# Sixteen taps of a second convolution group on TensorE, and the convolution's norm moved forward, in a two-layer streaming encoder

## The chip, the cores and the metric

The kernel runs on one core of a Trainium2 chip. The metric is the device time of one execution in microseconds; the median of several runs is given. The core has four engines that compute: TensorE (PE, with its weight loads PEld listed apart), VectorE (DVE), ScalarE (ACT) and GpSimd (POOL). SyncE (SP) only issues transfers here.

## What is computed

Two layers of a Conformer-like block over 512 tokens of width 1024: half a feed-forward block, a mixing block, half a feed-forward block, a norm. The mixing block projects the normed input once; part of the columns goes to an attention with low-rank queries and keys, the other part to a convolution module. Both results are joined and go through one output projection. The change is in the convolution module and what follows it:

```python
def conv_group(u_raw, conv_w, conv_b, ln_g, ln_b):
    a, g = u_raw[..., :CONV_W], u_raw[..., CONV_W:]
    u = a * jax.nn.sigmoid(g)
    y = lax.conv_general_dilated(u, conv_w[:, None, :], window_strides=(1,),
        padding=[(CONV_K - 1, 0)], feature_group_count=CONV_W, ...)   # depthwise, 31 taps, causal
    y = y + conv_b
    return jax.nn.silu(layer_norm(y, ln_g, ln_b))                     # norm over the 512 channels
...
x = x + jnp.concatenate([attn, conv], axis=-1) @ w_out[l]
```

## The kernel before

The stream `x` stays on the chip as eight tiles of 128 features by 512 tokens. Matrix products with weights are done in three parts (high x high, high x low, low x high, helper `mm3`, lines 158 to 160), so each block of 128 x 128 weights costs three matmuls over 512 tokens. The feed-forward blocks, which the change does not touch, fill most of the time.

The mixing block (`mix_body`) runs once per layer. The 512 convolution channels are four groups c = 0 to 3 of 128. `conv_in(c)` makes the gated input `u[c]` of a group (its last step is L640). The list `TAPS = (0, 31, 31, 0)` divides the 31 taps of each group between engines:

- groups 0 and 3: all taps on DVE, one `scalar_tensor_tensor` per tap into one PSUM bank (L956, tag `cv`, one bank for both groups one after the other), then a copy to SBUF by ACT (L964);
- group 1: a product per tap on ACT (L960, tile `pr`, four buffers) and an add per tap on POOL (L962);
- group 2 (`PC`): the first 16 taps on TensorE in `conv_pe` (L664), the other 15 as in group 1. For TensorE, `u[2]` is copied with shifts of 0 to 3 tokens by 16 transfers on SP's queue (L656) into four tiles `shifted`; 16 matmuls with diagonal 32 x 32 blocks (`diag`) then sum 16 taps, each a pair of records in the trace; ACT takes the result out with the bias (L666).

Attention goes over eight heads in a software pipeline. At step k it issues the transposes `turn(k)` (L836, L841), `scores(k-1)` (L860, maxima on DVE L864, exponents on ACT L868), `turn_p(k-3)` (L883, L886) and, for two heads at a time, `values` (L898, L901, L905, L908) and `turn_out`, which splits a result into high and low parts (L165, L166). `conv_pe` is put in front of step `PSTEP = 3`.

After the heads comes the convolution's norm over the 512 channels: the sum `ysum` of the four group results, two adds on POOL (L978, L979) and one on DVE (L980), in a buffer from the five shared `tmp` tiles; the mean by a matmul (L982); a subtraction per group (L988); squares on ACT (L188, L191) with adds on DVE (L195); the sum over channels by one-column matmuls (L202); the power -1/2 on POOL (L177); a diagonal on DVE (L217) that a matmul spreads to all channels (L221); a product per group (L998), the swish on ACT (L1000), and the split. The tables of ACT's functions are loaded for the exponents at L923 and for the swish at L984.

The output projection has eight column blocks, each a group of 8 x 3 matmuls: four over attention's results (`at`), four over the convolution's (`cv`). The attention halves of the first four blocks (`early_groups`) are issued between the steps of the norm.

The order on each queue is fixed when the program is built: a planner goes through a simulated timeline and gives an engine, at each moment, the ready instruction that comes first in the program (or has a higher priority). On the chip each queue runs in that order.

Of the kernel before, what the change touches and what calls it, by code (L numbers as in the profile page):

```python
# [15 lines left out]
P = 128  # L16
# [21 lines left out]
NP = 3  # L38
NC = 2
CHUNKS = ((0, 2), (2, 5), (5, 8), (8, 11))  # L40
TAPS = (0, 31, 31, 0)
Q = 32
PT = 16
PC = 2
PSTEP = 3
AHEAD = 2
PAUSE = 16
SEQ = "q0 R c1 q1 q2 qo k kt tt uq uk c2 c3"
# [3 lines left out]
EARLY = "s"  # L52
PRELOAD = 1
E1 = 1
E2 = 2
E3 = 3
WOG = 4
WAKE = 10
KS = (0, 2, 4, 6, 1, 3, 5, 7)
WOP = 4  # L60
# [2 lines left out]
JOINED = ("b21", "t3", "t4")  # L63

VECS = [("g1", 8), ("gm", 8), ("g2", 8), ("gp", 8), ("gql", 3), ("gkl", 2),
        ("cw", 4 * CK), ("cb", 4), ("lg", 4), ("lb", 4), ("gq", 1), ("gk", 1), ("cp", PT)]
VOFF = {}
_o = 0
for _n, _w in VECS:
# [9 lines left out]
def encoder_kernel(ctx: ExitStack, tc: tile.TileContext, xT, consts, vecs, rgain, wgu1, wd1, wdq1,  # L79
# [11 lines left out]
    def nm(s):  # L91
        uid[0] += 1
        return f"{s}{uid[0]}"
# [4 lines left out]
    def tmp(w=S, dt=FP):  # L98
        return tmps.tile([P, w], dt, tag="t", name=nm("t"))

    def bank():
        return psum.tile([P, S], FP, tag="ps", name=nm("ps"))

    def tiny(tag, w, dt=FP):
        return small.tile([P, w], dt, tag=tag, name=nm(tag))
# [73 lines left out]
    class Stats:  # L179


        def __init__(self):
            self.acc = self.tail = None

        def add(self, src, scale=1.0, last=False, eng=None, apart=False):
            if self.acc is None:
# [7 lines left out]
                return  # L194
            (eng or (V if last else G)).tensor_tensor(self.acc, self.acc, sq, ALU.add)  # L195

        def sums(self):
            ps = bank()
            parts = [self.acc] + ([self.tail] if self.tail is not None else [])
            for part in parts:  # L200
                for t in range(NT):
                    order["sums"] = T.matmul(ps[:, t:t + 1], part[:, t * P:(t + 1) * P], ones[:, 0:1],  # L202
                                             start=part is self.acc and (t == 0 or len(parts) == 1),
                                             stop=part is parts[-1], skip_group_check=len(parts) > 1).ins
            return ps[:, 0:NT]

        def token(self, n):
            self.ve = small.tile([P, NT], FP, tag="vtok", name=nm("vtok"), bufs=4)
            V.tensor_scalar(self.ve, self.sums(), 1.0 / n, EPS, ALU.mult, ALU.add)
# [4 lines left out]
    def spread(r):  # L214

        dg = tmp()
# [3 lines left out]
        ps = bank()  # L220
        order["spread"] = T.matmul(ps, ones, dg, start=True, stop=True).ins  # L221
        return ps

# [396 lines left out]

    def mix_body(kpool, l, gx, norm, done):
        u, order = [], {}
        diag = kpool.tile([P, PT, Q], FP, tag="m", name=nm("m"), bufs=11)
        G.tensor_tensor(diag, cst[:, None, CI32:CI32 + Q].to_broadcast([P, PT, Q]),
                        vv(l, "cp")[:, :, None].to_broadcast([P, PT, Q]), ALU.mult)
        shifted = []

        def kept(dt=FP):
            return kpool.tile([P, S], dt, tag="m", name=nm("m"), bufs=11)
        ys = [kpool.tile([P, S], FP, tag=f"y{c}", name=nm("y"), bufs=1) if n else None for c, n in enumerate(TAPS)]  # L630

        def glu(pa, pg):
            tg = tmp()
# [9 lines left out]
        def conv_in(c):  # L643
            pp = []
            for j in range(2):
                ps = bank()
                group(ps, load_w(wcv[l, 2 * c + j], WC, f"c{c}"), gx, range(KD), KD)
                pp.append(ps)
            glu(*pp)
            if c != PC:  # L650
                return
            for i in range(4):
                v = slot()
                V.memset(v[:, 0:4], 0.0)
                for r in range(4):
                    nc.sync.dma_start(out=v[r * Q:(r + 1) * Q, r:], in_=u[c][i * Q:(i + 1) * Q, 0:S - r])  # L656
                shifted.append(v)

        def conv_pe():

            ps = bank()
            for a in range(PT // 4):
                for i in range(4):
                    T.matmul(ps[i * Q:(i + 1) * Q, 4 * a:], diag[:, 4 * a + i], shifted[i][:, 0:S - 4 * a],  # L664
                             start=a == 0, stop=a == PT // 4 - 1)
            A.activation(ys[PC], ps, AF.Identity, bias=vv(l, "cb")[:, PC:PC + 1])  # L666

        gql, gkl = vv(l, "gql"), vv(l, "gkl")
        KW = KVL + DR
# [176 lines left out]
        def scores(h):  # L846
            qT, kT = heads[h]["qk"]
            b01, b2, b3 = bank(), bank(), bank()
            if h % 2 == 0:
                heads[h]["sums"] = small.tile([P, NT, 2], FP, tag="sums", name=nm("sums"), bufs=3)  # L850
            sums = heads[h - h % 2]["sums"]
            mx = small.tile([P, NT], FP, tag="mx", name=nm("mx"), bufs=3)
            pi = []
            ps = [slot() for _ in range(3)]
            ps = [ps[0][:, 0:128], ps[0][:, 128:384], ps[1][:, 0:384], ps[2]]
            for i in range(NT):
                n = (i + 1) * P
# [10 lines left out]
                A.activation(p, o, AF.Exp, bias=mx[:, i:i + 1], scale=scqs[i][:, h:h + 1] if QFOLD else 1.0,  # L868
                             accum_out=sums[:, i, h % 2:h % 2 + 1])
                pi.append(p)  # L870
            heads[h]["p"] = pi

# [70 lines left out]
        cw, cb = vv(l, "cw"), vv(l, "cb")  # L943
        for c, n in enumerate(TAPS):
            tap = lambda k: cw[:, c * CK + k:c * CK + k + 1]
            acc = psum.tile([P, S], FP, tag="cv", name=nm("cv"), bufs=1) if n < CK else None
            if n and c != PC:
                A.activation(ys[c], u[c], AF.Identity, scale=tap(CK - 1), bias=cb[:, c:c + 1])
            for s in range(n, CK):
                k = CK - 1 - s  # L950
# [3 lines left out]
                    A.activation(acc[:, s:], u[c][:, :S - s], AF.Copy, scale=tap(k))  # L954
                else:
                    V.scalar_tensor_tensor(acc[:, s:], u[c][:, :S - s], tap(k), acc[:, s:], ALU.mult, ALU.add)  # L956
            for s in range(PT if c == PC else 1, n):
                k = CK - 1 - s
                pr = kpool.tile([P, S], FP, tag="pr", name=nm("pr"), bufs=4)
                A.activation(pr[:, s:], u[c][:, :S - s], AF.Copy, scale=tap(k))  # L960
                with tc.issue_after(order["keys"]) if s >= PAUSE or c > 1 else nullcontext():
                    order["conv"] = G.tensor_tensor(ys[c][:, s:], ys[c][:, s:], pr[:, s:], ALU.add).ins  # L962
# [15 lines left out]
        G.tensor_tensor(ysum, ys[0], ys[1], ALU.add)  # L978
        G.tensor_tensor(ysum, ysum, ys[2], ALU.add)  # L979
        V.tensor_tensor(ysum, ysum, ys[3], ALU.add)  # L980
        pm = bank()
        T.matmul(pm, onesm, ysum, start=True, stop=True)  # L982
        if PRELOAD:
            A.activation(tiny("pre", 1), ysum[:, 0:1], AF.Silu)  # L984
# [293 lines left out]
```

## Time and profile before

| what | value |
|---|---|
| median of 3 runs | 1805.45 us (1805.23 to 1808.48) |
| the profiled execution | 1807.3 us, its span 1805.5 us |
| mean granted TensorE clock | 0.995 |
| PE busy in the span | 99% |
| DVE, ACT, POOL busy | 83%, 61%, 21% |
| the DVE steps of the taps (L956) | 120, 88.0 us busy |
| the POOL steps of the taps (L962) | 90, 120.7 us busy |

All times of the trace count from the start of the span. A row of the timeline gives start, length, engine, line, operation, and in brackets how long the engine was idle before and what ended that. A matmul is pipelined and its end is modelled, so a busy PE need not be a full one. The first mixing block lies at about 300 to 560 us, the second at about 1195 to 1455.

### The profile page before, as it was taken

The page shows a single profiled execution, that of the slowest core. Times are in us where ns is not written, and L with a number is a line of the kernel's source. Part 1 is how long each engine was busy: PE and PEld are TensorE (multiplying, and loading weights), DVE is VectorE, ACT ScalarE, POOL GpSimd, SP SyncE. Part 2 cuts the span into 40 slices and gives each one's busy share as a digit, 9 for nine tenths or more (in the row PEclk, how much of TensorE's full clock was granted, in tenths as well). Part 3 has the DMA queues.
Part 4 walks back from the last instruction along what each step waited for, and adds up shares of the span by engine and source line. Part 5 has one row for each costly group of instructions (what it writes and reads, how often), then busy time and mean ns, then how long its engine had stood idle before and what let it go on. Part 6 is the DMA issues. An engine that isn't in the chain of part 4 may idle for free.

```text
span 1805.5 us, 29455 instructions
## 1 busy us (share of the span) xinstructions
PE 1786.9 (99%) x11430; PEld 1585.0 (88%) x11430; DVE 1497.1 (83%) x2309; ACT 1094.3 (61%) x1699; POOL 381.4 (21%) x313
## 2 busy tenths in 40 slices
PE   9999999999999999999999999999999999999998
PEld 7899999888668899999888999998976788999997
DVE  7898988689945989898779989876998559989883
ACT  5575756467843575756645656554777435757564
POOL 1000000258623000000310000002685310000002
PEclk9999999999999999999999999999999999999999
DMA  4657574325203466665426575743260125575742
GB/s 167 167 135 188 128 182 116 107 88 134 54 12 111 115 163 161 158 158 135 123 64 169 125 191 125 191 108 117 74 174 3 36 88 159 142 177 138 179 120 73
DMA packets 71947, 228.28 MB, mean 126 GB/s; under 512 B 8448, under 2 KB 9600, under 8 KB 71808
## 3 DMA queue, kind: packets, MB, share of 16 engines
q1 hardware_dynamic: 55536, 171.87, 29.8%
q0 software_dynamic: 16128, 54.53, 17.6%
q8 instruction: 89, 1.46, 0.3%
q14 instruction: 50, 0.41, 0.1%
q10 hardware_dynamic: 144, 0.00, 0.0%
HBM read 222.19 MB, written 2.10 MB: 124 GB/s over the span
## 4 chain that ended last, share of the span: by engine, by line
PE 90%; DVE 4%; ACT 3%; POOL 1%; issue 1%; DMA 0%; SPq 0%; ACTq 0%; DVEq 0%; POOLq 0%
PE ps L158 23%; PE ps L160 23%; PE ps L159 23%; PE ps L377 11%; PE ps L378 6%; ACT pr L960 1%; PE ps L905 1%; ACT r L868 1%; PE ps L860 1%; PE ps L883 1%; PE ps L202 1%; POOL sck L177 1%; PE ps L898 0%; PE ps L221 0%; DVE kn L810 0%
## 5 line engine op out<-in xcount | busy, mean ns | idle before, releaser
L159 PE MATMUL ps<-r,wh 128*128 128x256 f32 (+1 forms) x2556 | 814.7, 319 | 0.5 <-DVE r L166 0.5
L158 PE MATMUL ps<-r,wh 128*128 128x256 f32 (+1 forms) x2556 | 811.6, 321 | 3.5 <-ACT r L165 1.5
L160 PE MATMUL ps<-r,wl 128*128 128x256 f32 (+1 forms) x2364 | 757.0, 322 | 0.0
L158 PEld LDWEIGHTS ps<-r,wh 128*128 128x128 f32 x2556 | 484.4, 190 | 50.1 <-ACT wh L142 3.4
L159 PEld LDWEIGHTS ps<-r,wh 128*128 128x128 f32 x2556 | 485.5, 190 | 37.5 <-DVE r L166 2.6
L160 PEld LDWEIGHTS ps<-r,wl 128*128 128x128 f32 x2364 | 449.0, 190 | 34.8 <-DVE wl L148 0.7
L377 PE MATMUL ps<-xj,wh 128*128 128x512 f32 x864 | 303.8, 391 | 0.0
L142 ACT CAST wh<-raw 128x1024 fp32r<-128x1024 f32 (+3 forms) x148 | 132.4, 901 | 210.2 <-PE ps L159 126.5
L248 ACT CAST wh<-fr 128x1024 fp32r<-128x1024 f32 (+1 forms) x160 | 157.6, 985 | 105.1 <-DVE fr L414 49.4
L148 DVE TENSOR_TENSOR wl<-raw,wh 128x1024 fp32r<-128x1024 f32 (+3 forms) x132 | 144.6, 1103 | 89.3 <-ACT wh L142 88.6
L394 POOL DMA_DIRECT2D ls<-in_wgu x72 | 62.5, 868 | 734.6 <-ACT ls L393 501.7
L250 DVE TENSOR_TENSOR wl<-fr,wh 128x1024 fp32r<-128x1024 f32 (+1 forms) x160 | 182.0, 1138 | 20.1 <-ACT wh L248 20.1
L377 PEld LDWEIGHTS ps<-xj,wh 128*128 128x128 f32 x864 | 161.4, 188 | 30.1
L378 PE MATMUL ps<-xj,ls 128*128 128x256 f32 x576 | 161.3, 280 | 0.0
L962 POOL TENSOR_TENSOR y<-y,pr 128x495 f32<-128x495 f32 (+29 forms) x90 | 120.7, 1342 | 46.6 <-ACT pr L960 41.0
L248 ACT CAST wh<-raw 128x1024 fp32r<-128x1024 f32 (+1 forms) x100 | 98.2, 982 | 45.3 <-PE ps L159 24.5
L250 DVE TENSOR_TENSOR wl<-raw,wh 128x1024 fp32r<-128x1024 f32 (+1 forms) x100 | 113.4, 1134 | 14.3 <-ACT wh L248 13.8
L378 PEld LDWEIGHTS ps<-xj,ls 128*128 128x128 f32 x576 | 108.3, 188 | 0.0
L393 ACT ACTIVATE ls<-fr 128x1024 fp32r<-128x1024 f32 (+1 forms) x56 | 56.1, 1002 | 75.4 <-PE ps L378 41.5
L195 POOL TENSOR_TENSOR r<-r,t 128x512 f32<-128x512 f32 x45 | 74.1, 1654 | 128.9 <-ACT t L191 128.2
L956 DVE SCALAR_TENSOR_TENSOR cv<-m,vec,cv 128x511 f32<-128x511 f32 (+14 forms) x120 | 88.0, 733 | 3.8 <-ACT cv L952 2.1
L484 DVE SCALAR_TENSOR_TENSOR x<-ps,x 128x512 f32<-128x512 f32 x112 | 76.8, 686 | 8.0 <-PE ps L160 7.4
(245 smaller groups left out, 2878.8 us busy)
## 6 DMA issues: line engine op xcount, KB each, us to landing
fr<-in_wgu SPq DMA_DIRECT2D x112, 512.0 KB, 4.2
ls<-in_wgu POOLq DMA_DIRECT2D x72, 512.0 KB, 6.1
raw<-in_wgu SPq DMA_DIRECT2D x62, 512.0 KB, 4.7
fr<-in_wdq SPq DMA_DIRECT2D x48, 384.0 KB, 4.7
ls<-in_wdq POOLq DMA_DIRECT2D x32, 384.0 KB, 4.7
raw<-in_wd SPq DMA_DIRECT2D x32, 384.0 KB, 3.1
raw<-in_wd SPq DMA_DIRECT2D x32, 256.0 KB, 2.7
raw<-in_wcv SPq DMA_DIRECT2D x16, 512.0 KB, 3.6
```

The costliest lines, as they stand in the source:

```text
L142: order["cast"] = A.copy(hi[:, :w], raw[:, :w]).ins
L148: (G if kind in POOLW.split() else V).tensor_tensor(lo[:, :w], raw[:, :w], hi[:, :w].bitcast(FP), ALU.subtract)
L158: T.matmul(o, lh, rh, start=first, stop=False, skip_group_check=free)
L159: T.matmul(o, lh, rl, start=False, stop=False, skip_group_check=free)
L160: order["mm"] = T.matmul(o, ll, rh, start=False, stop=last, skip_group_check=free).ins
L248: A.copy(hi[:, :w], src[:, :w])
L250: order["lo"] = V.tensor_tensor(lo[:, :w], src[:, :w], hi[:, :w].bitcast(FP), ALU.subtract).ins
L377: T.matmul(o, w[0][:, c], both, start=start and k == 0, stop=False, skip_group_check=True)
L378: last = T.matmul(o[:, 0:HS], w[1][:, c], both[:, 0:HS], start=False, stop=k == 3, skip_group_check=True).ins
L484: return V.scalar_tensor_tensor(v, o.rearrange("p (m t) -> p m t", m=2), 0.5 * sign, v, ALU.mult, ALU.add).ins
L956: V.scalar_tensor_tensor(acc[:, s:], u[c][:, :S - s], tap(k), acc[:, s:], ALU.mult, ALU.add)
L962: order["conv"] = G.tensor_tensor(ys[c][:, s:], ys[c][:, s:], pr[:, s:], ALU.add).ins
```

## The change

Group 3 gets the same division as group 2 for its first 16 taps: they go to TensorE, by 16 more shifting transfers and a second run of `conv_pe` in front of step 4. Its other taps stay on DVE, as one ACT step and 14 DVE steps into the bank, and one DVE add joins the two parts. The norm's steps, from `ysum` to the spread, are issued at a higher priority (`CHAIN = 400`); they no longer take `tmp` tiles and general PSUM banks but the tiles `u[1]` to `u[3]` and one `diag`, which are free by then, and the bank `cv`. The squares are not added up by DVE: four sets of one-column matmuls sum them on TensorE. The products and the swish are done in place. The load of the swish table and the swish itself are queued behind the last head's exponents, and the remaining three early groups are no longer interleaved with the norm. The tile pool `m` gets a twelfth buffer, `pr` three instead of four.

```diff
-TAPS = (0, 31, 31, 0)
+TAPS = (0, 31, 31, 16)
-PC = 2
-PSTEP = 3
+PC = (2, 3)
+PSTEP = {3: 2, 4: 3}
-E2 = 2
-E3 = 3
+CHAIN = 400
...
+    def behind(ins):
+        stack = ExitStack()
+        for i in ins:
+            stack.enter_context(tc.issue_after(i))
+        return stack
+
+    def conv_bank():
+        return psum.tile([P, S], FP, tag="cv", name=nm("cv"), bufs=1)
...
-        def sums(self):
-            ps = bank()
-            parts = [self.acc] + ([self.tail] if self.tail is not None else [])
+        def sums(self, made=bank):
+            ps = made()
+            parts = self.parts or [self.acc] + ([self.tail] if self.tail is not None else [])
...
-        diag = kpool.tile([P, PT, Q], FP, tag="m", name=nm("m"), bufs=11)
-        G.tensor_tensor(diag, cst[:, None, CI32:CI32 + Q].to_broadcast([P, PT, Q]),
-                        vv(l, "cp")[:, :, None].to_broadcast([P, PT, Q]), ALU.mult)
-        shifted = []
+        diag = {}
+        for i, c in enumerate(PC):
+            diag[c] = kpool.tile([P, PT, Q], FP, tag="m", name=nm("m"), bufs=12)
+            G.tensor_tensor(diag[c], cst[:, None, CI32:CI32 + Q].to_broadcast([P, PT, Q]),
+                            vv(l, "cp")[:, i * PT:(i + 1) * PT, None].to_broadcast([P, PT, Q]), ALU.mult)
+        shifted = {}
...
-            if c != PC:
+            if c not in PC:
                 return
+            shifted[c] = []
...
-            A.activation(ys[PC], ps, AF.Identity, bias=vv(l, "cb")[:, PC:PC + 1])
+            if ys[c] is None:
+                ys[c] = shifted[c][0]
+            A.activation(ys[c], ps, AF.Identity, bias=vv(l, "cb")[:, c:c + 1])
...
-            if step == PSTEP:
-                conv_pe()
+            if step in PSTEP:
+                conv_pe(PSTEP[step])
...
-                pr = kpool.tile([P, S], FP, tag="pr", name=nm("pr"), bufs=4)
+                pr = kpool.tile([P, S], FP, tag="pr", name=nm("pr"), bufs=3)
...
-        ysum = tmp()
-        G.tensor_tensor(ysum, ys[0], ys[1], ALU.add)
-        G.tensor_tensor(ysum, ysum, ys[2], ALU.add)
-        V.tensor_tensor(ysum, ysum, ys[3], ALU.add)
-        pm = bank()
-        T.matmul(pm, onesm, ysum, start=True, stop=True)
+        st = Stats()
+        with tc.high_priority(CHAIN):
+            ysum = u[1]
+            G.tensor_tensor(ysum, ys[0], ys[1], ALU.add)
+            G.tensor_tensor(ysum, ysum, ys[2], ALU.add)
+            V.tensor_tensor(ysum, ysum, ys[3], ALU.add)
+            pm = conv_bank()
+            T.matmul(pm, onesm, ysum, start=True, stop=True)
+            for c in range(4):
+                V.tensor_tensor(ys[c], ys[c], pm, ALU.subtract)
+                sq = (u[1], u[2], u[3], diag[2].rearrange("p a b -> p (a b)"))[c]
+                A.activation(sq, ys[c], AF.Square)
+                st.parts.append(sq)
+            r = st.token(CW, conv_bank)
+            pr = spread(r, conv_bank, u[1])
         if PRELOAD:
-            A.activation(tiny("pre", 1), ysum[:, 0:1], AF.Silu)
-        early_groups(range(E1, E2))
-        st = Stats()
-        for c in range(4):
-            V.tensor_tensor(ys[c], ys[c], pm, ALU.subtract)
-            st.add(ys[c], eng=V)
-        r = st.token(CW)
-        early_groups(range(E2, E3))
-        pr = spread(r)
-        early_groups(range(E3, WOG))
+            with behind(heads[H - 1]["exps"]):
+                A.activation(tiny("pre", 1), ysum[:, 0:1], AF.Silu)
+        early_groups(range(E1, WOG))
...
         for c in range(4):
-            z = tmp()
-            V.tensor_tensor(z, ys[c], pr, ALU.mult)
-            s = tmp()
-            A.activation(s, z, AF.Silu, bias=lb[:, c:c + 1], scale=lg[:, c:c + 1])
+            z = s = ys[c]
+            V.tensor_tensor(z, z, pr, ALU.mult)
+            with behind(heads[H - 1]["exps"]):
+                A.activation(s, z, AF.Silu, bias=lb[:, c:c + 1], scale=lg[:, c:c + 1])
             cv.append(split(s))
```

More of the change, by code (lines that the diff above doesn't have):

```diff
@@ L65 @@
 VECS = [("g1", 8), ("gm", 8), ("g2", 8), ("gp", 8), ("gql", 3), ("gkl", 2),
-        ("cw", 4 * CK), ("cb", 4), ("lg", 4), ("lb", 4), ("gq", 1), ("gk", 1), ("cp", PT)]
+        ("cw", 4 * CK), ("cb", 4), ("lg", 4), ("lb", 4), ("gq", 1), ("gk", 1), ("cp", 2 * PT)]
 VOFF = {}
@@ L183, in __init__ @@
             self.acc = self.tail = None
+            self.parts = []
         def add(self, src, scale=1.0, last=False, eng=None, apart=False):
@@ L202, in sums, with token @@
                     order["sums"] = T.matmul(ps[:, t:t + 1], part[:, t * P:(t + 1) * P], ones[:, 0:1],
-                                             start=part is self.acc and (t == 0 or len(parts) == 1),
+                                             start=part is parts[0] and (t == 0 or len(parts) == 1),
                                              stop=part is parts[-1], skip_group_check=len(parts) > 1).ins
             return ps[:, 0:NT]
-        def token(self, n):
+        def token(self, n, made=bank):
             self.ve = small.tile([P, NT], FP, tag="vtok", name=nm("vtok"), bufs=4)
-            V.tensor_scalar(self.ve, self.sums(), 1.0 / n, EPS, ALU.mult, ALU.add)
+            V.tensor_scalar(self.ve, self.sums(made), 1.0 / n, EPS, ALU.mult, ALU.add)
             r = small.tile([P, NT], FP, tag="rtok", name=nm("rtok"), bufs=4)
@@ L212, in token, with spread @@
             return r
-    def spread(r):
-        dg = tmp()
+    def spread(r, made=bank, dg=None):
+        dg = tmp() if dg is None else dg
         V.tensor_tensor(dg.rearrange("p (t j) -> p t j", t=NT),
@@ L219, in spread @@
                         r[:, :, None].to_broadcast([P, NT, P]), ALU.mult)
-        ps = bank()
+        ps = made()
         order["spread"] = T.matmul(ps, ones, dg, start=True, stop=True).ins
@@ L622, in mix_body @@
         u, order = [], {}
-        diag = kpool.tile([P, PT, Q], FP, tag="m", name=nm("m"), bufs=11)
-        G.tensor_tensor(diag, cst[:, None, CI32:CI32 + Q].to_broadcast([P, PT, Q]),
-                        vv(l, "cp")[:, :, None].to_broadcast([P, PT, Q]), ALU.mult)
-        shifted = []
+        diag = {}
[4 more added lines that the diff above has]
+        shifted = {}
         def kept(dt=FP):
-            return kpool.tile([P, S], dt, tag="m", name=nm("m"), bufs=11)
-        ys = [kpool.tile([P, S], FP, tag=f"y{c}", name=nm("y"), bufs=1) if n else None for c, n in enumerate(TAPS)]
+            return kpool.tile([P, S], dt, tag="m", name=nm("m"), bufs=12)
+        ys = [kpool.tile([P, S], FP, tag=f"y{c}", name=nm("y"), bufs=1) if 0 < c < 3 else None for c in range(4)]
         def glu(pa, pg):
@@ L656, in conv_in, with conv_pe @@
                     nc.sync.dma_start(out=v[r * Q:(r + 1) * Q, r:], in_=u[c][i * Q:(i + 1) * Q, 0:S - r])
-                shifted.append(v)
-        def conv_pe():
+                shifted[c].append(v)
+        def conv_pe(c):
             ps = bank()
@@ L663, in conv_pe @@
                 for i in range(4):
-                    T.matmul(ps[i * Q:(i + 1) * Q, 4 * a:], diag[:, 4 * a + i], shifted[i][:, 0:S - 4 * a],
+                    T.matmul(ps[i * Q:(i + 1) * Q, 4 * a:], diag[c][:, 4 * a + i], shifted[c][i][:, 0:S - 4 * a],
                              start=a == 0, stop=a == PT // 4 - 1)
-            A.activation(ys[PC], ps, AF.Identity, bias=vv(l, "cb")[:, PC:PC + 1])
+            if ys[c] is None:
+                ys[c] = shifted[c][0]
+            A.activation(ys[c], ps, AF.Identity, bias=vv(l, "cb")[:, c:c + 1])
         gql, gkl = vv(l, "gql"), vv(l, "gkl")
@@ L867, in scores @@
                     V.tensor_tensor(mx[:, i:i + 1], mx[:, i:i + 1], scqs[i][:, h:h + 1], ALU.mult)
-                A.activation(p, o, AF.Exp, bias=mx[:, i:i + 1], scale=scqs[i][:, h:h + 1] if QFOLD else 1.0,
-                             accum_out=sums[:, i, h % 2:h % 2 + 1])
+                heads[h].setdefault("exps", []).append(A.activation(p, o, AF.Exp, bias=mx[:, i:i + 1], scale=scqs[i][:, h:h + 1] if QFOLD else 1.0,
+                             accum_out=sums[:, i, h % 2:h % 2 + 1]).ins)
                 pi.append(p)
@@ L945, in mix_body @@
             tap = lambda k: cw[:, c * CK + k:c * CK + k + 1]
-            acc = psum.tile([P, S], FP, tag="cv", name=nm("cv"), bufs=1) if n < CK else None
-            if n and c != PC:
+            acc = conv_bank() if n < CK else None
+            if n and c not in PC:
                 A.activation(ys[c], u[c], AF.Identity, scale=tap(CK - 1), bias=cb[:, c:c + 1])
@@ L956, in mix_body @@
                     V.scalar_tensor_tensor(acc[:, s:], u[c][:, :S - s], tap(k), acc[:, s:], ALU.mult, ALU.add)
-            for s in range(PT if c == PC else 1, n):
+            for s in range(PT if c in PC else 1, n):
                 k = CK - 1 - s
-                pr = kpool.tile([P, S], FP, tag="pr", name=nm("pr"), bufs=4)
+                pr = kpool.tile([P, S], FP, tag="pr", name=nm("pr"), bufs=3)
                 A.activation(pr[:, s:], u[c][:, :S - s], AF.Copy, scale=tap(k))
@@ L1239 @@
     put("cw", a["conv_w"].reshape(L, CK, 4, P).transpose(3, 0, 2, 1).reshape(P, L, 4 * CK))
-    cp = a["conv_w"][:, ::-1][:, :PT, PC * P:(PC + 1) * P].reshape(L, PT // 4, 4, 4, Q)
-    put("cp", cp.transpose(2, 4, 0, 1, 3).reshape(P, L, PT))
+    cp = a["conv_w"][:, ::-1][:, :PT, PC[0] * P:].reshape(L, PT // 4, 4, len(PC), 4, Q)
+    put("cp", cp.transpose(2, 5, 0, 3, 1, 4).reshape(P, L, len(PC) * PT))
     for name, key in (("gq", "q_norm"), ("gk", "k_norm")):
```

## Prediction

> **What bounds the kernel now.** I read the page first: its span, the busy shares and the chain that ended last.
>
> ```profile
> span 1805.5 us, 29455 instructions
> PE 1786.9 (99%) x11430; PEld 1585.0 (88%) x11430; DVE 1497.1 (83%) x2309; ACT 1094.3 (61%) x1699; POOL 381.4 (21%) x313
> PE 90%; DVE 4%; ACT 3%; POOL 1%; issue 1%; DMA 0%; SPq 0%; ACTq 0%; DVEq 0%; POOLq 0%
> ```
>
> TensorE sets the time, but a tenth of the chain lies on other engines. The change touches only the mixing block, which runs twice, so I cut that block into stages in the table of windows (columns: stretch, its length, then PE, PEld, DVE, ACT, POOL busy, granted clock, DMA). The cuts are where the chain changes engine: the conv inputs end at 449.6, the attention's first part ends at 474.9, its second at 506.3, then comes the conv norm, then the output projection. The first three rows are stages of the first layer, two show the clock where it falls, one is a full stretch to compare with, and the last is the second layer's norm.
>
> ```profile
> 449.60:474.90 25.30, 24.74 (x196) 14.82 (x194) 24.51 (x47) 25.30 (x62) 23.17 (x20) 1.00 0.42 110
> 474.90:506.30 31.40, 31.34 (x266) 21.45 (x266) 25.16 (x50) 19.58 (x52) 9.45 (x8) 1.00 0.01 2
> 506.30:522.20 15.90, 12.96 (x41) 9.40 (x42) 7.30 (x12) 4.56 (x7) 1.03 (x1) 0.79 0.00 1
> 514.00:515.00 1.00, 0.00 (x0) 0.00 (x0) 0.90 (x2) 0.00 (x0) 0.00 (x0) 1.00 0.00 0
> 515.00:516.00 1.00, 0.82 (x4) 0.85 (x5) 0.03 (x1) 0.00 (x0) 0.00 (x0) 0.52 0.00 0
> 540.00:550.00 10.00, 10.00 (x45) 8.20 (x44) 9.49 (x6) 5.56 (x8) 10.00 (x5) 1.00 0.42 143
> 1400.20:1416.10 15.90, 12.97 (x41) 9.35 (x42) 7.31 (x12) 4.56 (x7) 1.03 (x1) 0.79 0.00 0
> ```
>
> The norm stage is the same to a few hundredths in both layers, so I work out one layer and double it. In the first part of attention ACT is never idle; in the second PE is never idle; in the norm stage nobody is full and the TensorE clock is 0.79. That stage is what the change is about. The chain of waits, in order of time (start, length, what), shows why:
>
> ```profile
> 474.92 1.09 PE ps L898 x16
> ...
> 506.41 0.70 DVE t L908
> ...
> 509.26 1.07 PE ps L982 x2
> ...
> 514.34 0.70 DVE r L195
> 515.18 1.84 PE ps L202 x8
> 517.02 0.64 PE ps L158
> ...
> 522.18 0.87 PE ps L221 x2
> ```
>
> The mean (L982), the centring (L988), the sums of squares (L195 on DVE, L202 on PE) and the spread of the result (L221) come one after another after the last head, and PE waits in them. The timeline gives the ends of this tail, the holes and the slow matmuls:
>
> ```profile
> 496.89 1.28 POOL L978 TENSOR_TENSOR t<-m,y 128x512 f32<-128x512 f32 x1 [14.71 <-DVE r L166]
> 506.23 0.50 PE L158 MATMUL ps<-r,wh 128*128 128x512 f32 x1
> 507.77 1.28 ACT L984 ACT_TABLE_LOAD   x1
> 507.80 0.49 PE L158 MATMUL ps<-r,wh 128*128 128x512 f32 x1 [0.61 <-ACT r L165]
> 508.39 0.68 DVE L980 TENSOR_TENSOR t<-t,m 128x512 f32<-128x512 f32 x1
> 508.53 0.50 PE L159 MATMUL ps<-r,wh 128*128 128x512 f32 x1 [0.23 <-DVE r L166]
> 512.70 0.39 PE L160 MATMUL ps<-r,wl 128*128 128x512 f32 x1
> 518.31 0.63 PE L158 MATMUL ps<-r,wh 128*128 128x512 f32 x1
> 518.73 0.63 PE L159 MATMUL ps<-r,wh 128*128 128x512 f32 x1
> 559.24 0.39 PE L160 MATMUL ps<-r,wl 128*128 128x512 f32 x1
> ```
>
> The output projection is 8 column blocks of 8 x 3 = 192 matmuls. Six of them run before 506.23; the other 186 run from 506.23 to 559.47 (the last starts at 559.24 and takes one spacing of 0.23), 53.2 us. Unhindered, a matmul of this shape takes 10.00/44 = 0.227 us (the row of 540 to 550, 45 records of which one straddles an edge), so 186 need 42.3. **The tail holds 10.9 us per layer beyond its own matmuls.** Named: L982, L202 and L221 take about 0.9 + 1.8 + 0.9 = 3.6; between 512.70 and 515.18 PE stands 2.2; the clock is halved from about 515 (1.00, then 0.52) and from 517.0 to 522.2 twelve matmuls have a spacing of 0.42 (518.31 to 518.73) in place of 0.227, 2.4; waiting for the last head's split, at 507.80 and 508.53, costs 1.3 beyond the normal spacing; 1.4 are small.
>
> L978 and L980 also show that the norm is late by order, not by need: POOL could have begun the sum of the four conv outputs 14.71 us earlier, and stood for a temporary buffer; DVE's part, L980, then stood behind the last head's split.
>
> **What the change does to the tail.** The sum goes into u[1], which no one else needs; the chain gets a higher priority, so the planner puts it between the attention's steps. The last inputs it needs are POOL's conv taps and the last group's accumulator on DVE:
>
> ```profile
> 458.94 23.25 POOL L962 TENSOR_TENSOR y<-y,pr 128x484 f32<-128x484 f32 x18
> L956 DVE SCALAR_TENSOR_TENSOR cv<-m,vec,cv 128x511 f32<-128x511 f32 (+14 forms) x120 | 88.0, 733 | 3.8 <-ACT cv L952 2.1
> 474.90:506.30 31.40, 9.98 (x14) 1.00 0.01 2
> ```
>
> (The short row is the window of L956 alone.) POOL's taps end at 482.2. The accumulator chain of the last group, 30 steps on DVE, still has 14 to do at 474.9; with 16 taps on PE it has one ACT step and 14 DVE steps, so it should be done by about 475. From 482.2 the chain needs two POOL adds (2.6), a DVE add, the mean, four subtractions (2.7), squares on ACT (19.58 of 31.40 busy, so there is room), sums, POOL's power, the diagonal, the spread and four products: about 17 us if nothing waited, 25 with the attention in between, so ready near 500 to 508. The early projection groups, 48 matmuls or 10.9 us, cover until 517. So I take the tail as 42.3 plus the last head's split 1.3, plus 0.6 of small holes: 44.2. **Gain 9.0** (7.5 if a product or the swish is late, 10.3 if other groups fill the split's hole).
>
> **What it adds to attention.** On PE the mean and the spread (0.9 each) move in, and the sums: four parts in place of one, 32 records. At full clock eight took 0.95:
>
> ```profile
> 401.00:402.20 1.20, 0.95 (x8) 0.92 (x8) 1.00 0.00 0
> 456.61 3.60 PE L664 MATMUL ps<-r,m 128*32 128x512 f32 x32
> 464.75 0.60 PE L836 MATMUL ps<-cst,q 128*96 128x128 f32 x4
> ```
>
> so 4 x 0.8 = 3.2 without the last one's drain, and 5.0 in all. The page's PE row (31.34 of 31.40) would charge all 5.0, the weight loads (21.45 of 31.40 against 8.20 of 10.00 in a full stream) would let nearly all of it fall into holes. I charge half, **2.5**, with 0 and 5.0 as ends. [...]
>
> The other addition is the second run of tap matmuls: 3.60 us of PE by its sibling. It goes ahead of step 4, so before the transposes at 464.75, in the part where ACT is full and PE's weight loads are at 14.82 of 25.30. Ends 0 and 3.6; I take **1.5**, nearer the holes. Its inputs come by 16 more DMAs on SP:
>
> ```profile
> 446.87 1.33 DVE L640 TENSOR_TENSOR m<-t,t 128x512 f32<-128x512 f32 x1
> 437.66 15.33 SPq L656 DMA_DIRECT2D r<-m  x16
> DMA to landing us min/median/max: 2.0/4.7/6.5
> ```
>
> The last gate product is there at 448.2, but SP is with the third group's 16 shifts until 453.0; the last eight of those, from 446.2, took 0.86 each, so the new ones end between 463 (0.6 each, as the shorter ones) and 467, and the last lands 2 to 4.7 later: 465 to 471, where PE wants it near 465. If late, PE stands with scores and transposes behind it, ACT's exponents behind these. I charge **0.5** (0 to 5). What SP has queued behind, weights of projection blocks not used before 517, can wait.
>
> DVE loses 16 steps of 0.733, 11.7 us per layer, and gets one add and four memsets. DVE was 24.51 of 25.30 busy in the first part, but ACT ended the waits, so I book **-0.3** (-2 to 0). ACT gets the eviction of the new taps in place of the copy out of the accumulator, moved into its full part: **0.3**, at most one activation. The tap products have three buffers instead of four; POOL, 23.17 of 25.30 busy, paces them, and I leave a delay in the next term.
>
> That term is standing: the queues run in order, and the planner fixed the order from its own durations. Where a chain step comes to the head of a queue before its input is there, DVE's maxima, PE's transposes and through them ACT's exponents stand behind it. The trace of before has no such place inside attention, so I bound it: 0 if the planner's times hold, 6.6 if three pending tap adds (23.25/18 = 1.3 each) and the two POOL adds (1.28 each) are all waited for. I take **1.5**, near the low end, because POOL follows ACT's products closely: it finished them at 482.2 and ACT, which makes them, never stood between 449.6 and 474.9.
>
> Squares beside exponents: no square runs under attention's function table in this trace. They run without a reload behind the load of 507.77, so I charge 0. If each of the four needed a load before and one behind, 8 x 1.28 = 10.2 per layer would be added to ACT; that end I hold for so unlikely that it has no case of its own.
>
> **Sum.** Per layer -9.0 + 2.5 + 1.5 + 0.5 - 0.3 + 0.3 + 1.5 = -3.0, for two layers -6.0. Against the profiled run (1807.3, span 1805.5, 1.8 outside the span) that is 1801.3 with a span of 1799.5; against the median of 1805.45 it is **1799.5**. The profiled run is 1.9 above the median and within the three runs.
>
> **Rivals.** (1) *Attention swallows it all.* The added PE work falls into holes, no one stands, the split's hole is filled: -9.6 + 1.0 + 1.0 + 0.6 = about -7 per layer, 1791.5. For it: PEld at 68% and 59%. Against: PE is busy for 31.34 of 31.40 us in the second part.
>
> (2) *The clock falls inside attention.* Now it falls at about 515.0, after PE stood 2.2 us behind 6 us of stop and go. With three stands and 32 one-column matmuls this can move into attention and cost the same 2.4 per layer: -0.6 per layer, 1804.3. Against: squares come one by one, with attention between, and eight alone at 401 left the clock at 1.00. [...]
>
> (3) *Slower: the chain stands at the head of the queues.* The whole 6.6 is waited for, and the clock falls behind that wait: -3.0 - 1.5 + 6.6 + 2.4 = +4.5 per layer, 1814.5. It decides from 4.5 us of standing per layer on, where the gain is gone. For it: DVE waits for POOL before the keys today, and POOL has no slack until 482. Against: ACT's products pace POOL.
>
> (4) *The chain is not early after all.* A late tap, accumulator or buffer keeps the norm behind the last head. Then only DVE's three square adds (2.1) go, while sums (2.4), taps (1.5) and the DMA term (0.5) stay: +2.3 per layer, 1810.
>
> **Chances.** Forecast 0.40, (1) 0.12, (2) 0.16, (3) 0.22, (4) 0.10. A difference under 0.2%, 3.6 us, can hardly be told from none; so faster 0.52, same 0.16, slower 0.32. The range 1790 to 1815 takes in (1) to (4); what is left out is one term at its end in both layers: a late landing with a full charge on PE above, a DVE relief of 2 below.
>
> **What would show it.** Right: L980 and L982 before the last head's split, no stage with the clock under 0.95, 186 projection matmuls within 45 us, attention (449.6 to 506.3) longer by 4 to 8 us. Wrong: a wait over 2 us in front of the new L664 (landing), of the mean or the sums (standing), a table load between exponents, or a norm that still begins behind the last head. If attention grew by more than 9 us, the forecast's sign is wrong.

## The result and the profile after

The changed kernel takes 1810.83 us in the median (1808.04 to 1813.14), the kernel before 1805.54 beside it (1802.14 to 1808.48). The ratio is 1.0031, with a 95% interval of 1.0021 to 1.004. It is slower, by 5.3 us or 2.7 per layer, where 6 us of gain were forecast. The profiled run took 1810.84, its span 1808.9. The time of the kernel before goes with its mean granted clock: of its 79 executions beside the experiments the six at 1.000 took 1800.2 to 1801.2 and the ten at 0.995 1806.9 to 1808.6, its profiled one stands at 0.995, and all ten of the changed kernel stand at 0.996 or 0.997.

First the page of the changed kernel: span, busy shares, chain.

```profile
span 1808.9 us, 29704 instructions
PE 1797.3 (99%) x11542; PEld 1592.8 (88%) x11542; DVE 1475.2 (82%) x2281; ACT 1095.6 (61%) x1699; POOL 381.1 (21%) x315
PE 92%; DVE 3%; ACT 2%; POOL 2%; issue 1%; DMA 0%; SPq 0%; ACTq 0%; POOLq 0%; DVEq 0%
```

DVE lost 21.9 us of work and PE got 10.4, and the chain lies on PE for 92% in place of 90%. The relieved engine was not the one that set the time. The windows of the changed kernel (stretch, length, then PE, PEld, DVE, ACT, POOL, granted clock, DMA) show attention's second part, the place where the clock falls, the tail, and the same place in the second layer:

```profile
474.90:506.30 31.40, 31.40 (x247) 23.95 (x247) 20.35 (x43) 21.87 (x56) 9.59 (x8) 0.90 0.01 2
499.00:500.00 1.00, 1.00 (x11) 1.00 (x11) 0.00 (x0) 0.00 (x0) 0.00 (x0) 1.00 0.00 0
500.00:501.00 1.00, 1.00 (x7) 1.00 (x7) 0.00 (x0) 0.00 (x0) 0.00 (x0) 0.52 0.00 0
520.00:560.00 40.00, 40.00 (x177) 32.79 (x176) 22.05 (x21) 17.02 (x24) 17.83 (x9) 1.00 0.24 70
1398.00:1404.00 6.00, 6.00 (x34) 4.56 (x36) 2.29 (x6) 3.13 (x6) 1.03 (x1) 0.50 0.00 0
```

The tail is now a full stream: 177 matmuls in 40.00 us, 0.226 each, the clock at 1.00 and no hole. But the low clock has moved. At 500 it drops from 1.00 to 0.52 although PE was busy for the whole of both microseconds, and the second layer has the same at 1398. The chain of the changed kernel, in order of time, says what PE did there:

```profile
456.32 3.60 PE ps L676 x32
...
464.62 3.52 PE ps L676 x30
...
468.66 1.02 PE ps L676 x2
...
484.93 1.31 PE ps L897 x10
...
490.95 0.86 PE cv L998 x2
...
497.15 4.25 PE cv L211 x32
501.40 0.88 PE ps L874 x4
...
502.38 4.53 PE ps L897 x20
506.91 0.90 PE cv L230 x2
...
514.11 0.43 PE ps L166
...
520.18 0.43 PE ps L166
```

L998, the mean, is at 490.95, ahead of the last heads: the norm did move forward. But the 32 one-column matmuls (L211) are one block of 4.25 us, and they stand in front of the last head's scores (L874). Behind the block, 20 transposes (L897) take 4.53 us, where ten of them took 1.31 at 484.93. The timeline shows who stood behind it:

```profile
501.44 0.16 DVE L218 TENSOR_SCALAR vtok<-cv 128x4 f32<-128x4 f32 x1 [4.55 <-PE cv L211]
503.02 0.47 ACT L882 ACTIVATE r<-ps,mx 128x256 f32<-128x256 f32 x1 [5.42 <-DVE mx L878]
```

VectorE stood for 4.55 us and ScalarE, with the last head's exponents to do, for 5.42.

**A ledger of the first layer.** The last gate product ended at 448.20 before; now it ends at 448.60. The last value matmuls were done, and the projection ran alone, from 506.23 before and from 520.18 now. Taking out the projection matmuls that run ahead of that (6 before; 14 now, counted by their lines in the trace; 0.227 each), attention grew from 58.0 - 1.4 = 56.7 us to 71.6 - 3.2 = 68.4: by 11.7. The rows above nearly add up to it: second tap run 3.6 by its sibling (up to 4.5 by its own two rows), block 4.25, mean 0.86, spread 0.90, slow transposes 4.53 - 2 x 1.31 = 1.9, together 11.5 to 12.4. The tail lost its whole 10.9. That leaves +0.8. From the last gate product to the last addition to `x` the trace shows the same:

```profile
446.25 2.35 DVE L651 TENSOR_TENSOR m<-t,t 128x512 f32<-128x512 f32 x1 [1.25 <-ACT t L647]
562.00 0.68 DVE L1029 TENSOR_TENSOR x<-x,ps 128x512 f32<-128x512 f32 x1
```

562.68 - 448.60 = 114.1 us, against 561.58 - 448.20 = 113.4 before (its last addition starts at 560.90 and takes 0.68). The second layer gives 115.5 against 113.9. The two layers' 2.3 us are most of the 3.4 between the spans. The spans differ by less than the medians because the profiled run of before was a long one, 1807.3, with the clock's fall in both of its norm stages. The 10.9 us of its tail hold that fall.

### The profile page after: what moved, and what is told of

Its sections match the earlier page's. It is cut to its first block, busy times and chain, and to the rows that moved or that the text cites. A ratio compares the mean times of both kernels' runs of the same rounds, so it can differ in the third digit from the quotient of the medians.

```text
span 1808.9 us, 29704 instructions
## 1 busy us (share of the span) xinstructions
PE 1797.3 (99%) x11542; PEld 1592.8 (88%) x11542; DVE 1475.2 (82%) x2281; ACT 1095.6 (61%) x1699; POOL 381.1 (21%) x315
## 4 chain that ended last, share of the span: by engine, by line
PE 92%; DVE 3%; ACT 2%; POOL 2%; issue 1%; DMA 0%; SPq 0%; ACTq 0%; POOLq 0%; DVEq 0%
PE ps L166 23%; PE ps L167 23%; PE ps L168 22%; PE ps L386 11%; PE ps L387 6%; PE ps L874 1%; PE ps L897 1%; PE ps L919 1%; PE ps L676 1%; POOL y L976 1%; ACT pr L974 1%; PE ps L912 1%; PE cv L211 0%; POOL sck L185 0%; ACT wh L150 0%
## 5 line engine op out<-in xcount | busy, mean ns | idle before, releaser
L403 POOL DMA_DIRECT2D ls<-in_wdq x32 | 27.6, 863 | 261.6 <-ACT ls L402 261.6
```

Source lines behind the costliest of these rows:

```text
L403: G.dma_start(out=lo[:, :n], in_=w, accum_op=ALU.add)
```

## The experiments

Ratios are to the kernel before, run beside each experiment on the same chip (medians of before 1803.8 to 1804.7). A hundredth of a per cent is 0.18 us, 0.09 per layer. Most ratios are good to about 0.001, so the difference of two of them is good to about 0.0013, which is 1.2 us per layer; with the taps alone it is 0.0015 to 0.0019.

**VectorE adds the squares.** The changed kernel, but with 8 one-column matmuls in place of 32:

```diff
-                st.parts.append(sq)
+                if c:
+                    V.tensor_tensor(u[1], u[1], sq, ALU.add)
+                else:
+                    st.parts.append(sq)
```

> The kernel after, with one thing undone: the four squares are added by VectorE (three adds of about 0.7 us) and TensorE sums one part, 8 records in place of 32. Theory S (sums): in the trace of after the 32 one-column matmuls stand in one block of 4.3 us in front of the last head's scores, and the TensorE clock falls behind them; 24 records less give 2.4 to 3.2 us and the clock's fall about 3 us per layer, so about 11 us in all: 1799 to 1802, clock 1.00 through attention. Theory T (taps): the second run of tap matmuls (3.6 us) and its late transfers (2.0 us of waiting) are what costs; then only the 24 records themselves go, 1806 to 1809. Theory C (crowding): every step put into attention is paid in full and DVE's three adds are paid too: about 1808 to 1811.

1800.81 us, 0.9982 (0.9973 to 0.999). One edit turns the change from slower to faster: 0.49%, 4.4 us per layer, as Theory S said. The gain over before is no more than before itself has at a clock of 1.000 (1800.2 to 1801.2, against 1799.0 to 1802.1 here, with clocks of 0.998 to 1.000), so much of it may be the clock; that is not shown. The timeline has

```profile
499.46 1.05 PE L211 MATMUL cv<-ones,m 128*128 128x1 f32 x8
500.37 0.85 PE L897 MATMUL ps<-cst,r 128*128 128x128 f32 x6
```

and the mean clock of the run is 0.999.

**The taps alone.** The kernel before with the taps of group 3 divided as in the change (`TAPS`, `PC`, `PSTEP`, the shifts, three `pr` buffers), its norm unchanged.

> The kernel before with only the taps moved: 16 taps of group 3 on TensorE, the norm as before at its old place. Theory S: the taps cost little, since attention's first part has holes on PE and DVE is relieved: 1804 to 1809. Theory T: 3.6 us of matmuls and 2.0 us of waiting are paid in both layers: about 1815 to 1817. Theory C: the 3.6 us are paid, the waiting partly: 1811 to 1815.

1811.34 us, 1.0043 (1.0028 to 1.0058): 3.9 us per layer lost (Theory C), as much as the tap run's own PE time: 3.6 us where it runs undivided, 4.5 in step 4, where the planner put scores of 0.5 us in front of its last pair and that pair alone then takes 0.96. The edit also brings 16 more transfers and takes one `pr` buffer; no run separates these from the matmuls. This profile is of the slowest of the six runs, 1816.48. In it the clock also falls during the first tap run (0.66 from 455 to 460), after PE had stood twice for ScalarE, 0.73 and 0.50 us. The profile of the first experiment has nearly the same two waits (0.71 and 0.50) and a clock of 1.00, so I have no cause for that. The second tap run isn't the cause: the profile of "No taps, VectorE adds" below has the same 0.66 without one.

**The norm alone.** The changed kernel without the taps of group 3 on TensorE (`TAPS = (0, 31, 31, 0)`, `PC = (2,)`; one square gets another buffer).

> The kernel after without the taps: all 31 taps of group 3 on VectorE again, the norm's steps still at a higher priority in their own buffers and the squares still summed by TensorE. The last group's accumulator then ends near 495 us as before, so the norm comes about 7 us later than in after. Theory S: the 32 records and the clock's fall stay, 1805 to 1812. Theory T: without the taps 5.6 us per layer are won against after: about 1800. Theory C: 3.6 us per layer less than after, about 1804.

1806.76 us, 1.001 (1.0 to 1.002), as Theory S said: with the 32 one-column matmuls in it the clock falls in both layers (0.83 from 510 to 520, 0.76 from 1400 to 1410). VectorE's taps end at 496.09, so the mean is late:

```profile
495.37 0.72 DVE L970 SCALAR_TENSOR_TENSOR cv<-m,vec,cv 128x482 f32<-128x482 f32 x1
500.55 1.13 PE L998 MATMUL cv<-m,onesm 128*128 128x512 f32 x2
```

**One part summed.** Only the last group's square goes into the sum; the other three are left out of it, so 8 matmuls remain and VectorE adds nothing.

```diff
-                st.parts.append(sq)
+                if c == 3:
+                    st.parts.append(sq)
```

> The kernel after, but only the square of the last group is summed (the other three squares are made and left out of the sum): 8 one-column records in place of 32, and no adds on VectorE. Theory S: as the run with VectorE's adds or a little better, 1798 to 1801; the difference between the two is what the adds cost. Theory T and C: 1805 to 1809.

1800.46 us, 0.9982 (0.9974 to 0.9991): the same as with VectorE's additions (Theory S). So these cost nothing that can be measured, and the 24 extra matmuls, with the clock's fall behind them, are the whole difference.

**The same 32 matmuls, 128 columns wide.** Is it the instructions or what the array does in them?

```diff
-                    order["sums"] = T.matmul(ps[:, t:t + 1], part[:, t * P:(t + 1) * P], ones[:, 0:1],
+                    order["sums"] = T.matmul(ps[:, t * wide:(t + 1) * wide], part[:, t * P:(t + 1) * P], ones[:, 0:wide],
```

> The kernel after, with the 32 matmuls of the sums 128 columns wide in place of one: the same weight loads in the same places, the other 127 columns are not read. In after the granted clock fell to 0.50 after 3 us of one-column matmuls although PE was busy all that time. Theory K (clock): columns, not instructions, keep the clock up; then it stays at 1.00 through attention, the block lasts about 3.7 us (0.117 per record as the transposes), and 2.5 us per layer are won against after: about 1804 to 1806. Theory B (block): the 4.3 us for which scores stand behind the block are all of the cost and the clock falls anyway or does not matter: as after, 1809 to 1811.

1805.74 us, 1.0005 (0.9996 to 1.0014). The timeline and the window of the block:

```profile
497.28 3.84 PE L212 MATMUL cv<-ones,m 128*128 128x128 f32 x32
501.63 2.40 PE L898 MATMUL ps<-cst,r 128*128 128x128 f32 x20
501.00:506.00 5.00, 5.00 (x48) 3.93 (x48) 4.15 (x10) 3.66 (x8) 1.03 (x1) 1.00 0.00 2
```

The block of the same instructions with 128 times the columns kept the clock at 1.00, and the 20 transposes behind it took 2.40 instead of 4.53. The ratio falls by 0.0026, 2.3 us per layer, each of its eleven runs has a mean clock of 0.998 or more, and Theory K holds. That is the price of the clock, known to about 1.2 us. What remains to the first experiment, 1.0005 - 0.9982, is 2.1 us per layer for the 24 instructions themselves, known no better.

**The block behind the last head's transposes.**

```diff
-            r = st.token(CW, conv_bank)
+            with tc.issue_after(heads[H - 1]["t"]):
+                r = st.token(CW, conv_bank)
```

> The kernel after, with the 32 one-column matmuls, the step on VectorE behind them and the power queued behind the last head's transposes (for each engine behind that matmul on TensorE: only the matmuls are moved). Theory B: the last head's scores no longer stand, 3 to 4 us per layer are won, the norm comes later but the early projection groups cover it: 1800 to 1804. Theory K: the 32 one-column matmuls still lower the clock, now over full-width matmuls, so about 2.4 us per layer of the gain are lost again: 1805 to 1809.

1805.25 us, 1.0001 (0.9992 to 1.001). That lies in the range of Theory K. Nobody's exponents wait for the block now, but in the first layer the clock still falls behind it:

```profile
503.98 3.63 PE L211 MATMUL cv<-ones,m 128*128 128x1 f32 x32
507.54 1.96 PE L912 MATMUL ps<-cst,rs 128*64 128x128 f32 x16
508.00:512.00 4.00, 4.00 (x27) 2.35 (x26) 0.69 (x1) 2.07 (x3) 0.92 (x1) 0.62 0.01 2
```

These rows are of the first layer; whether the clock falls in the second too is not shown. The mean clock of the profiled run is 0.998, where the changed kernel with two falls has 0.996, and its time, 1802.29, is well below the median. So the 0.3% that is won against the changed kernel was the place in front of the scores, or which work met the low clock, or that the clock falls less often here (0.996 to 0.999 over the eleven runs); this run doesn't tell these apart.

**No taps, VectorE adds.** The norm alone, with the edit of the first experiment.

> The kernel after without the taps and with the squares added by VectorE: only the early norm in its own buffers is left. If the taps cost 1 to 2 us per layer even beside the early norm (as the run without taps against after, 2.6 us in all), this is 1797 to 1799. If the taps are what makes the early norm possible (the accumulator ends near 495 us without them), the norm comes too late and this is 1801 to 1804.

1802.13 us, 0.9986 (0.9977 to 0.9995): the second of the two cases. The mean comes at 502.80, against 490.91 with the taps at step 4. There the ratio was 0.9982, so the taps bring nothing that can be measured: the earlier norm that they allow just pays for their matmuls.

**The second tap run at step 6.** The first experiment with `PSTEP = {3: 2, 6: 3}`.

> As the run with VectorE's adds (1800.8 there), but the second run of tap matmuls stands in front of step 6 in place of step 4. If its price is its place in the stretch where ACT was full and PE is now full (the next transposes came 5.0 us later than in the run without taps), a later place changes little: 1800 to 1802. If late transfers cost 2 us per layer, 1796 to 1798. If the sum of the four groups waits for it, 1802 to 1805.

1796.97 us (1796.53 to 1797.24), 0.9955 (0.9943 to 0.9968): faster than both kernels. The same window of the first experiment, then of this one:

```profile
465.00:470.00 5.00, 5.00 (x40) 1.40 (x35) 3.47 (x7) 3.50 (x9) 4.69 (x5) 1.00 0.92 314
```

```profile
465.00:470.00 5.00, 5.00 (x42) 3.45 (x42) 5.00 (x12) 5.00 (x16) 4.69 (x5) 1.00 0.86 308
477.67 3.60 PE L676 MATMUL ps<-r,m 128*32 128x512 f32 x32
486.82 1.02 PE L998 MATMUL cv<-m,onesm 128*128 128x512 f32 x2
```

At step 4 the tap run starves ScalarE and VectorE (3.50 and 3.47 of 5.00); at step 6 both are full in that stretch, and the mean comes at 486.82, 4.1 us earlier. The tap run also stands undivided here, 3.60 us, where step 4 had taken 4.5: about 1 us less of PE in each layer. The time lies in the range that was named for late transfers, but that number is not borne out as a cause: the first experiment's profile shows no wait of PE for a transfer. I took the gain for a cost of the place and tried it in the two other kernels.

**Step 6, squares summed by TensorE.** The changed kernel, with that one edit.

> The changed kernel with its squares still summed by TensorE, and only the second run of tap matmuls moved from step 4 to step 6. Theory P (the place of the tap run is a cost of its own): the move saved 0.9982 - 0.9955 = 0.27%, 4.9 us, where VectorE added the squares; it should save the same here: about 1806, ratio 1.0004, and turn(4)'s transposes start about 5 us earlier than in the changed kernel, near 464.6. Rival B (the two costs share one room): the block of 32 sums and the tap run then meet in the second half of attention, and the move saves under 2 us: 1809 to 1812, ratio over 1.002.

1808.9 us, 1.0024 (1.0014 to 1.0033): only 0.07% less than the changed kernel, and the intervals overlap. Turn(4)'s transposes do start earlier, at 464.21, as Theory P said, but its time is not won (Rival B). The block of sums now follows at once on the mean, and the clock falls behind it again:

```profile
491.57 3.73 PE L211 MATMUL cv<-ones,m 128*128 128x1 f32 x32
495.00:496.00 1.00, 1.00 (x9) 0.90 (x9) 0.16 (x1) 0.00 (x0) 0.42 (x1) 0.61 0.00 0
```

**Step 6, the taps alone.** The second experiment with the later step.

> The kernel before with only the taps of the last group moved to TensorE, the norm as it was, and the second tap run in front of step 6 in place of step 4. The taps alone at step 4 cost 1.0043. Theory P: the place was the larger part of that, so 1.0043 - 0.0027 = 1.0016, about 1807.5: what stays is tap matmuls on a full TensorE without an earlier norm to pay for them. Rival F (the matmuls cost the same wherever they stand): 1.003 to 1.005, 1810 to 1814.

1812.41 us, 1.0041 (1.0029 to 1.0053), against 1.0043 at step 4. No price of the place shows (0.02%, known to 0.19%), as Rival F said: here the tap run costs its full 3.7 us per layer at both steps. It is divided here too, 1.06 and 3.58 us with scores between. Of the three kernels a later run pays clearly only in the one with an early norm and no block of sums.

**Both tap runs a step later**, 4 and 7.

> The fastest kernel so far with both tap runs a step later, 4 and 7 in place of 3 and 6. Theory A (ScalarE must have tap products to do when TensorE turns to its tap run, and a later run meets that less well, while the group results come later): 1798 to 1803, mean after 490. Rival L (the later the better, since the first part of attention is where ScalarE is full): 1793 to 1796.

1803.65 us, 0.9995 (0.9986 to 1.0004). The second run starts at 482.28 and the mean comes at 495.02, so most of the gain is gone. The first run now waits 0.40 us for ScalarE and takes 4.26 us in place of 3.60, and the second is divided again. "The later the better" falls.

**No higher priority.** The kernel of step 6 with the norm's steps at their ordinary priority, their buffers kept.

```diff
-        with tc.high_priority(CHAIN):
+        with nullcontext():
```

> The fastest kernel so far (squares added by VectorE, second tap run at step 6, 1796.97) without the higher priority of the norm's steps; the buffers of their own stay. Theory Q (the priority brings the norm forward): without it the mean stands behind the last head's transposes or values again, after 505, and its gain of the tail goes: 1801 to 1806, ratio 0.998 to 1.001. Rival R (the buffers do it: the planner gives a ready step to an idle engine anyway): 1795 to 1799, ratio 0.994 to 0.997, the mean still before 495.

1796.04 us (1795.75 to 1796.85), 0.9948 (0.9936 to 0.996); the mean is at 486.24. The priority does nothing here that can be measured, as Rival R said. That the buffers of their own do it is what remains of the change to the norm, but no run took them away. This is the lowest median of the kernels measured, not to be told from that with the priority.

## Why the prediction was wrong

**The step that failed is the charge for PE work in attention.** The prediction had two rows side by side, PE busy 31.34 of 31.40 and the weight loads 21.45 of 31.40, and charged half of the added 5.0 us for the norm's matmuls (2.5) and 1.5 of 3.6 for the taps. The runs show that all of it was to be charged. The taps alone cost 3.7 to 3.9 per layer; the mean, the spread and the block stand in the chain with 0.86, 0.90 and 4.25. The row that said so was PE's own: charged in full, the prediction's own sum is +1.6 per layer, 1808.7. I had read the weight-load row as room for added matmuls, and the measurement speaks against that reading. The holes in the weight-load row (21.45 of 31.40 busy) took up nothing that shows, and the block is itself weight loads without a gap (PEld 1.00 of 1.00 in 499 to 500).

**Rival 2 happened on top of that, and I had put it aside for a wrong reason.** "Squares come one by one, with attention between": they do, on ScalarE; their sums do not. All 32 matmuls go into one bank as one group, and the planner left them together. "Eight alone left the clock at 1.00" was true of eight, 0.95 us long; the 32 take 4.25. The rival's price, 2.4 per layer, fits (2.3 by the wide matmuls, known to 1.2). It named the 32 matmuls beside three stands as the trigger; the stands were not needed, PE was busy throughout (31.40 of 31.40 us). Its 1804.3 was 6.5 too low since it kept the half charges.

**The other terms.** The tail was sized 1.9 too low: 10.9 gained, not 9.0, since other work also filled the split's hole. *Transfers:* the last shift was issued by 463.1 and PE shows no gap in front of the second tap run, so 0 in this profile; that of "One part summed" has one wait of 1.25 us for a landing, within the first layer's second tap run (from 449.6 to 474.9 PE is busy for 22.82 us there, 24.09 in the first experiment). *Standing* (1.5) was not what the term meant: PE waits for no step of the chain; VectorE and ScalarE stand behind the block (4.55 and 5.42 us). *Squares beside exponents* needed no table load: the timeline of 490 to 505 has the four squares, from 492.57 on, between exponents and no load. *VectorE's relief*: its additions could come back for nothing (one part summed, 0.9982 both ways), so the squares were moved off an engine that had room. With 9.0 put at 10.9, and all that was added put at the measured 11.7, the sum of the first layer is +0.8 in place of -3.0.

The points to watch held in part. The mean lies before the last head's split, and the projection is dense, as forecast. "No stage with the clock under 0.95" failed (0.90 in 474.9 to 506.3). Attention grew by 11.7, past the 9 at which the prediction said that its sign is wrong. Rivals 3 and 4 did not occur. That rival 4's time, 1810, is within 1 us of the measured one is luck: its norm stays behind the last head, and here the norm moved forward.

**What stays open.** The step of the second tap run is worth 0.27% in one kernel, 0.07% in another and 0.02% in a third, each known to 0.13 to 0.19%. So that it needs a short early norm is likely, not shown; why it is worth that much then is open too. Of its 4.9 us (3.8 by the two medians themselves, which are of two chips) only some 2.2 lie in the mixing blocks of the two profiles, and 1.9 of these are the undivided tap run (twice 0.96). Also open is the 0.66 clock during the first tap run.

## What to carry to other kernels

Where PE's busy row is full (here 31.34 of 31.40 us) and its queue runs in order, charge added matmuls in full (here 3.6 us of taps cost 3.9 per layer), and put them only where a hole is shown; a weight-load share of 68% was no hole here. Don't relieve an engine that has room by giving the bound one many tiny instructions (here the squares on TensorE cost 0.49%). Small edits interact: the taps cost 0.4% alone and bring up to 0.3% beside an early norm, so an edit is to be tried in the company that it will have. Where two kernels differ by a few tenths of a per cent, look at their mean granted clocks too (the kernel before took 1800.2 to 1801.2 at 1.000 and 1806.9 to 1808.6 at 0.995).

## What was not expected of the hardware

In the stream of 32 one-column matmuls the clock fell, from 1.00 in 499 to 500 to 0.52 in 500 to 501, though PE and its weight loads were busy for 1.00 of each microsecond. From the start of the block to the fall it took 2.9 us in the changed kernel (497.1 to 500.0), 3.3 in its second layer (1394.4 to 1397.7), and 3.6 in the first layer of each of two kernels in which the block stands elsewhere (it starts at 491.57 and 503.98; the fall is worked out from the mean clock of the microsecond that it cuts, 0.61 for 495 to 496, 0.80 for 507 to 508, and a low clock of 0.50). These are four blocks; the spread may be wider. The low stretches that the windows show whole are of two lengths, by the same working and to about 0.1: 6.8 us in both layers of the changed kernel and in both norm stages of before, 3.4 in the first layers of the other three kernels with the block; and where it falls without the block, 3.4 in the first tap run of two runs (0.66 from 455 to 460 in both), and 3.4, 6.8 and 6.9 in the first-layer norms of "No taps, VectorE adds" and of the taps alone at steps 6 and 4. The same 32 instructions with 128 columns took about as long (3.84 us against 3.63, 3.73, 3.78 and 4.32) and kept it at 1.00 from 449.6 to 525, and its eleven runs have a mean clock of 0.998 to 1.000. That the clock falls behind such a stream of single columns was shown here, by the wide matmuls; why it falls, and why it stays low for these two lengths, was not shown.
